# A hybrid decoder trunk: four plain tiles for six in the first up projection, its norm under the fourth product, and a last norm from two banks

## The chip, the cores and the metric

The kernel runs on one core of a Trainium2 chip. A core has TensorE (PE, matrix products; its weight loads are shown apart as PEld), VectorE (DVE), ScalarE (ACT), GpSimd (POOL) and SyncE (SP, which issues transfers). Each engine works through its own list of instructions in the order in which they were written down; semaphores make one engine wait for another. Transfers (DMAs) are issued by SP, POOL or ACT and run beside the engines. The metric is the device time of one execution in microseconds (us), taken as the median of several runs. All times below are microseconds unless they are marked ns.

## The reference

One layer over 512 positions of width 1024, batch 1, everything in float32:

```python
x = x + 0.5 * swiglu(rmsnorm(x, ffn1_norm), ffn1_wg, ffn1_wu, ffn1_wd)
x = x + hybrid_mixer(rmsnorm(x, mix_norm), ...)
x = x + 0.5 * swiglu(rmsnorm(x, ffn2_norm), ffn2_wg, ffn2_wu, ffn2_wd)
return rmsnorm(x, final_norm)

def rmsnorm(x, g):
    return x * lax.rsqrt(jnp.mean(x * x, axis=-1, keepdims=True) + EPS) * g

def swiglu(x, w_gate, w_up, w_down):      # w_gate, w_up: 1024 x 2816, w_down: 2816 x 1024
    return (jax.nn.silu(x @ w_gate) * (x @ w_up)) @ w_down
```

The mixer (sparse attention, a gated recurrence, two merge gates and an output projection) is not touched by the change. The final norm is.

## The kernel before

**Numbers in two parts.** Every float32 operand is split into a rounded part (`h`, made by ACT) and the rest (`l`, made by DVE as the difference, `wsplit`). A product of two such operands is three matmuls: h by h, h by l, l by h (`mm3`). The rounded type is `F32R`.

**The first up projection** works on tiles of 128 of the 2816 columns, so there are 22 tiles, each with a gate product (j = 0) and an up product (j = 1). The input lies transposed: `x[k]` holds 128 channels by 512 positions, eight of them. The first norm is not applied ahead of the products. The products take `y[k]`, which is `x[k]` by the norm's weight; the factor per position, `rstd`, is multiplied onto the results. `norm_steps` forms it: matmuls with a constant matrix `mean` on `acc` (the sum of squares, formed by ACT and DVE), a square root on ACT, a reciprocal on DVE, four transposes on PE that spread the factor over the partitions, and a copy to `rstd` by ACT.

The order is this:
1. Three products (both of tile 0, the gate of tile 1) are formed while x and their weights arrive (banks `WP`, weights `WS`), and a fourth (`pu`, the up product of tile 1) follows with weights from `AH[0]`. These banks wait until `rstd` is there; then `ffn_act` makes the activations of tiles 0 and 1.
2. `ffn_up` begins with plain tiles ("direct"). Each is two products of 8 x 3 matmuls of 512 positions (`gemm`). There are DIRECT = 4 of them, tiles 2 to 5, so eight products. With tiles 0 and 1 this makes six plain tiles (PLAIN = 6, which is also what the down projection is laid out for).
3. The other 16 tiles go in pairs through a scheme of Strassen and Winograd's kind: two tiles, two halves of the channels and two halves of the positions make a 2 x 2 problem with seven products in place of eight. Each of the seven products is 4 x 3 matmuls of 256 positions. This part is called the stream. `stream` lists its products as (p, w), with p the kind of product and w counting gate and up of each pair. Products of kinds 2, 5 and 3 are "wide" from the third w on: one weight load serves both halves of the operand.

**The operands of the stream.** Seven operands, four tiles each, are formed from the normed input and used by every pair: `n11` (for p = 1), `b21` (2), `t2` (6), `t1` (5), `r` (7), `q` (4) and `n22` (3). `moving_operands` forms them in four parts j: two scaled inputs `ca` and `cb` (DVE, with `rstd`), differences of their halves (DVE), and for each operand tile a rounded half (ACT, tile `cm`) and the rest. The rest is made in one of two ways. For n11, n22 and the last t1 and t2, DVE forms it. For the others ACT writes the negative of the source and a transfer issued by POOL adds the source onto it (`G.dma_start(..., accum_op=ALU.add)`).

**Banks.** Products 1, 6, 7 and 4 of one w add into one bank (`o.beta`), and between them `results` takes the partial sum out. After product 1, ACT copies the bank to `t1`; product 6, two places later in the stream, may add to the bank only after this copy.

**Queues around the change.** In `ffn_up` the order on every engine is written by hand (`tc.manual_schedule`). In the plain part each product is issued in two halves, and between and after the halves stand: the results of the product before (`results_direct`), the split of the weights two products ahead (`prepare_direct`), and a piece of operand forming. The stream's loop issues, for each i, `products(i)`, `results(i - 1)`, `prepare(i + LEAD)` with LEAD = 4 (the split of the weights four products ahead, and weight sums where p is 6 or 3), and at times a load. A load of one w (`load`) is four transfers on SP and two adding transfers on POOL. Raw weights have three buffers, split weights three.

**The end.** The second down projection leaves rows of 128 positions by 512 columns. Its last TAIL = 3 steps are issued for row block m = 0, then for m = 1. After them come, for each m, the addition of the last bank to the residual rows (DVE), the sum of squares (ACT for m = 0, DVE for m = 1), root, reciprocal, two scalings, and two output transfers of 128 x 512.

Of the kernel before, what the change touches and what calls it, by code (L numbers as in the profile page):

```python
# [14 lines left out]
P = 128  # L15
S = 512
# [26 lines left out]
WARM = 8  # L43
HS = S // 2
LEAD = 4
PLAIN, PAIRS, TAIL = 6, 8, 3
DIRECT = 4
WIDE, FIRST_WIDE = (2, 5, 3), 2

# [128 lines left out]
def hybrid_kernel(ctx, tc, xt, vec, w1u, w1d, wm, wki, wrg, watt, wrnn, wout, w2u, w2d, gf, out):  # L178
# [21 lines left out]
    def nm(s):  # L200
        cnt[0] += 1
        return f"{s}_{cnt[0]}"
# [34 lines left out]
    def wsplit(r, h, l):  # L237
        A.activation(h, r, AF.Copy)
        V.tensor_sub(l, r, f(h))
# [77 lines left out]
    def moving_operands(g):  # L317
# [28 lines left out]
        for j in range(KD // 2):  # L346
# [20 lines left out]
            moved("q", q)  # L367
            yield

    def ffn_act(pg, pu):  # L370
# [7 lines left out]
    def ffn_up(y, wu, n0, hs, g, waiting=(), given=(), ahead=None):  # L378

# [2 lines left out]


        H = KD // 2 * P
        f0 = n0 + DIRECT
        count = KF - f0
        ws = []

# [60 lines left out]
        stream = []  # L451
        for w in range(count):
            stream += [(1, w), (2, w)] + [(4, w - 1)] * (w > 0) + [(6, w)]
            stream += [(3, w - 1)] * (w > 0) + [(5, w), (7, w)]
        w = count - 1
        stream[-3:] = [(5, w), (7, w), (3, w - 1), (4, w), (3, w)]
        units = []
# [47 lines left out]

        def wide(p, w):

            return p in WIDE and FIRST_WIDE <= w < count - 2 * (p != 2)

        def results(i):  # L510
            p, w = stream[i]
# [25 lines left out]
            elif p == 3:  # L537
# [7 lines left out]
                else:  # L545
                    A.activation(o.t1, o.t1, AF.Silu)

        with tc.manual_schedule(engines=ENGINES):
            for _ in range(len(raws), RAWS + len(raws)):
                fetch()  # L550
            together(prepare_direct(), prepare_direct())
            operands, norm = moving_operands(g), norm_steps(acc)
            for d, (n, j) in enumerate(direct):
                sums.append(psum(("aux", "mm")[n % 2]))
                if d == 1:
                    norm_rest(norm)
                    hs.extend(ffn_act(*p) for p in waiting)
                gemm(sums[d], split_[d], y, range(KD), last=False, upto=KD // 2)
                steps = [results_direct(d - 1)] if d else []
                if d + 2 < len(direct):  # L560
                    together(prepare_direct(), *steps)
                    fetch()
                else:
                    together(*steps)
                    for i in range(2):
                        prepare(2 * (d + 2 - len(direct)) + i)
                if d == 0:
                    for _ in range(3):
                        next(norm)
                if d in (4, 6):  # L570
                    load_ = load(len(ws))
                if d >= 4:
                    next(load_, None)
                if d > 1:
                    next(operands, None)
                gemm(sums[d], split_[d], y, range(KD), first=False, since=KD // 2)
                if d > 1:
                    next(operands, None)
            for _ in operands:
# [200 lines left out]
    for r, src in zip(AH, (w1u[1, 1], w1u[2, 0], w1u[2, 1], w1u[3, 0])):  # L780
        Q.dma_start(r, src)

    def given(r):
        h, l = (wsp.tile([P, WMAX], F32R, tag=t, name=nm(t)) for t in ("wh", "wl"))
        wsplit(r, h, l)
        return h, l

    y = []
    for k in range(KD):
        y.append(norm_tile(k, V_G1, False))  # L790
        if k % CH == 0:
            c = slice(k * P, (k + CH) * P)
            for r, h, l in WS:
                wsplit(r[:, c], h[:, c], l[:, c])
        for i in range(3):
            mm3(WP[i], WS[i][1:], slice(k * P, (k + 1) * P), y[k], k == 0, k == KD - 1)
    pu, w = psum(), given(AH[0])
    for k in range(KD):
        norm_sum(k)
    gemm(pu, w, y, range(KD))  # L800
    hs = []

    sums = []
    d1 = block_down(hs, w1d, sums)
    ffn_up(y, w1u, 2, hs, V_G1, ((WP[0], WP[1]), (WP[2], pu)), AH[1:], d1.tasks_at)

    cc = const.tile([P, 8], F32, name="cc")
    hb = vt[:, V_BX:V_BX + 8]
# [802 lines left out]
            banks[key] = psum("aux" if p == 2 else "mm")  # L1611
        return banks[key]

    def products(i, ms=range(2)):
        h, l = (t[:, i % 2 * S:(i % 2 + 1) * S] for t in units[i // 2])
# [12 lines left out]
        t, starts = turned[p, j], p in (1, 2, 5)  # L1628
        opens = dict(skip_group_check=not starts)
        for m in ms:  # L1630
            o, th, tl = chain(p, m), t[:, m * QB:(m + 1) * QB], t[:, HS + m * QB:HS + (m + 1) * QB]
            T.matmul(o, th, h, start=starts and j == 0, stop=False, **opens)
# [81 lines left out]
    ffn_up(y2, w2u, 0, hs, V_G2, ahead=tasks_at)  # L1714
    with tc.manual_schedule(engines=ENGINES):
        assert min(d2.tasks) >= 0
        for i in range(len(steps) - TAIL):
# [11 lines left out]
        results(len(steps) - TAIL - 1)  # L1729
        assert not late  # L1730

        for m in range(2):
            for i in range(len(steps) - TAIL, len(steps)):
                products(i, (m,))
        for m in range(2):
            r = rows(m, 1)
            if m:
                norm_root(0)
            V.scalar_tensor_tensor(r, chain(4, m), 0.5, r, op0=ALU.mult, op1=ALU.add)
            squares(m, 1, norms[m][:, 2:3], (A, V)[m])  # L1740
        scaled(0, nc.scalar)
        norm_root(1)
        scaled(1, nc.scalar)


def _tiles(w, kt, m=P):
# [55 lines left out]
```

## Time and profile before

| | |
|---|---|
| median of 3 runs | 1063.96 us (1063.28 to 1064.0) |
| profiled execution | 1063.79 us |
| its span, first to last instruction | 1062.0 us |
| PE busy | 1052.5 us, 99% of the span |
| DVE, ACT, POOL busy | 83%, 63%, 16% |
| first matmul of the three first products | 4.85 us |
| rstd written by ACT | 35.88 us |
| first matmul of the first stream | 73.79 us |
| first matmul of the first down projection | 234.34 us |
| last matmul issued | 1054.28 us |

How to read the rows that follow later. A row of a timeline has the start in us from the beginning of the span, the length in us, the engine, the line of the kernel (L172 is the helper through which nearly every instruction is written, so the names of the tiles tell more than the line), the operation, what it writes <- what it reads, the shapes, and xN where N like instructions in a row were merged. In square brackets stands how long the engine was idle ahead of it and which work ended that wait. Matmuls overlap, so the distance between two starts is what one costs, not its length. A row of windows has the stretch, its length, PE's busy time (and instructions), the clock that PE was granted as a share of the full one, the share of the transfer engines in use, and GB/s. Buffer names have no numbers: `cm` is any operand tile of the stream, `wh` and `wl` the two parts of split weights, `tg` and `h` what the results are taken into, `ca` and `cb` the scaled inputs.

### The profile page before, as it was taken

The page shows a single profiled execution, that of the slowest core. Times are in us where ns is not written, and L with a number is a line of the kernel's source. Part 1 is how long each engine was busy: PE and PEld are TensorE (multiplying, and loading weights), DVE is VectorE, ACT ScalarE, POOL GpSimd, SP SyncE. Part 2 cuts the span into 40 slices and gives each one's busy share as a digit, 9 for nine tenths or more (in the row PEclk, how much of TensorE's full clock was granted, in tenths as well). Part 3 has the DMA queues.
Part 4 walks back from the last instruction along what each step waited for, and adds up shares of the span by engine and source line. Part 5 has one row for each costly group of instructions (what it writes and reads, how often), then busy time and mean ns, then how long its engine had stood idle before and what let it go on. Part 6 is the DMA issues. An engine that isn't in the chain of part 4 may idle for free.

```text
span 1062.0 us, 17140 instructions
## 1 busy us (share of the span) xinstructions
PE 1052.5 (99%) x6068; PEld 926.2 (87%) x6068; DVE 879.4 (83%) x1734; ACT 665.3 (63%) x1311; POOL 171.5 (16%) x219
## 2 busy tenths in 40 slices
PE   9999999999999999999999999999999999999997
PEld 7889999999999888888888888888899999998885
DVE  6687898889978889899989867756878988878885
ACT  6575555555656668897896574446656555565753
POOL 0161111102430002110100000001611111101510
PEclk9999999999999999999999999999999999999999
DMA  7297677738993464343423211434977777548973
GB/s 279 60 258 184 175 197 175 186 107 235 259 206 97 132 172 124 105 124 106 138 80 99 81 31 54 143 112 110 247 188 172 189 197 165 154 120 257 256 160 120
DMA packets 73239, 165.98 MB, mean 156 GB/s; under 512 B 9024, under 2 KB 15296, under 8 KB 73152
## 3 DMA queue, kind: packets, MB, share of 16 engines
q1 hardware_dynamic: 46608, 119.72, 34.7%
q0 software_dynamic: 26112, 44.58, 24.2%
q8 instruction: 48, 0.79, 0.3%
q10 hardware_dynamic: 432, 0.57, 0.2%
q14 instruction: 39, 0.32, 0.1%
HBM read 151.73 MB, written 2.10 MB: 145 GB/s over the span
## 4 chain that ended last, share of the span: by engine, by line
PE 98%; DMA 0%; issue 0%; ACT 0%; DVE 0%; SPq 0%; ACTq 0%
PE mm L172 68%; PE aux L172 29%; DMA x<-xt 0%; ACT wh L172 0%; ACT yh L172 0%; SPq L160 0%; DVE o L172 0%; DVE yl L172 0%; DVE xr L172 0%; DVE acc L172 0%; DVE sq L172 0%; ACT sq L172 0%; DVE rs L172 0%; ACTq L172 0%; DVE ss L172 0%
## 5 line engine op out<-in xcount | busy, mean ns | idle before, releaser
L172 PE MATMUL mm<-cm,wh 128*128 128x256 f32 x1472 | 268.5, 283 | 0.0
L172 PEld LDWEIGHTS mm<-cm,wh 128*128 128x128 f32 x1472 | 229.1, 191 | 3.4 <-ACT tg L172 0.2
L172 DVE TENSOR_TENSOR wl<-wr,wh 128x512 fp32r<-128x512 f32 (+2 forms) x228 | 188.9, 832 | 45.9 <-ACT wh L172 44.2
L172 PE MATMUL mm<-cm,wl 128*128 128x256 f32 x736 | 208.4, 283 | 0.0
L172 ACT ACTIVATE wh<-wr 128x512 fp32r<-128x512 f32 (+3 forms) x230 | 167.9, 737 | 56.6 <-issue 21.5
L172 PE MATMUL mm<-yh,wh 128*128 128x512 f32 (+1 forms) x416 | 163.7, 394 | 0.7 <-ACT wh L172 0.7
L172 PE MATMUL mm<-yl,wh 128*128 128x512 f32 (+1 forms) x416 | 162.3, 390 | 0.0
L172 PE MATMUL aux<-cm,wh 128*128 128x512 f32 (+1 forms) x552 | 159.6, 351 | 0.0
L172 PE MATMUL mm<-yh,wl 128*128 128x512 f32 x408 | 159.2, 390 | 0.0
L172 PEld LDWEIGHTS mm<-cm,wl 128*128 128x128 f32 x736 | 140.4, 191 | 0.0
L172 ACT ACTIVATE wh<-s 128x512 fp32r<-128x512 f32 x152 | 92.9, 624 | 54.4 <-DVE s L172 42.1
L172 DVE TENSOR_TENSOR wl<-s,wh 128x512 fp32r<-128x512 f32 x152 | 103.5, 686 | 24.9 <-ACT wh L172 23.2
L172 PE MATMUL aux<-cm,wl 128*128 128x256 f32 x440 | 123.7, 281 | 0.0
L172 PEld LDWEIGHTS aux<-cm,wh 128*128 128x128 f32 x552 | 96.7, 189 | 12.8 <-DMA cm<-cb 0.2
L172 PEld LDWEIGHTS mm<-yh,wh 128*128 128x128 f32 (+1 forms) x416 | 77.9, 187 | 17.8 <-ACT wh L172 1.4
L172 PEld LDWEIGHTS mm<-yl,wh 128*128 128x128 f32 (+1 forms) x416 | 77.6, 187 | 16.0 <-DVE yl L172 0.8
L172 PEld LDWEIGHTS mm<-yh,wl 128*128 128x128 f32 x408 | 76.6, 188 | 16.5 <-DVE wl L172 0.2
L172 PEld LDWEIGHTS aux<-cm,wl 128*128 128x128 f32 x440 | 83.5, 190 | 0.0
L172 PE MATMUL mm<-wh,cm 128*128 128x512 f32 x192 | 59.1, 389 | 0.0
L172 ACT ACTIVATE tg<-tg 128x512 f32<-128x512 f32 (+1 forms) x44 | 24.1, 548 | 50.8 <-DVE tg L172 50.8
L160 POOL DMA_DIRECT2D s<-w2u x36 | 33.6, 1063 | 125.1 <-DVE wl L172 47.0
L160 POOL DMA_DIRECT2D cm<-cb x8 | 7.1, 888 | 266.3 <-DMA wr<-w2u 209.1
(243 smaller groups left out, 2063.7 us busy)
## 6 DMA issues: line engine op xcount, KB each, us to landing
wr<-wm SPq DMA_DIRECT2D x39, 512.0 KB, 3.6
wr<-w2u SPq DMA_DIRECT2D x26, 512.0 KB, 4.7
wr<-w1u SPq DMA_DIRECT2D x21, 512.0 KB, 5.4
wr<-w1d SPq DMA_DIRECT2D x18, 512.0 KB, 4.4
s<-w2u SPq DMA_DIRECT2D x36, 256.0 KB, 6.0
s<-w2u POOLq DMA_DIRECT2D x36, 256.0 KB, 5.1
wr<-w2d SPq DMA_DIRECT2D x18, 512.0 KB, 5.4
s<-w1u SPq DMA_DIRECT2D x32, 256.0 KB, 5.7
```

The lines of the kernel that those rows point to most:

```text
L160: return self.engine.dma_start(out, src, **kw)
L172: return call(*args, **kw)
```

## The change

- The last two slices of the three first products are issued bank by bank: both slices of the first bank, then both of the second, then of the third.
- The fourth product moves into `ffn_up` (`first_tiles`). The mean's matmuls stand ahead of it, the transposes in its middle.
- There are two direct tiles in place of four (`plain` = 2), so four plain tiles in all and 18 in the stream. The loads of the first two w are issued ahead of the plain products.
- The operands are formed by `operand_parts` in the order of use: n11, b21, t2 and t1 in four parts among the plain products (the activations of tiles 0 and 1 among them, `act_steps`), then r, q and n22, one tile at a time, the first three behind the last plain product's halves and the others one for each i of the stream's loop. r and q are now subtracted in place from `ca` and `cb`.
- The stream takes the gate and the up of the first pair together: 1, 2, 6, 5 of each, then 7, 4 and 3 of both.
- At the end four steps are left for the tail. Row block 1 is formed in halves of 256 columns; the four steps of the second half go to a bank of their own (`rest`). Additions, sums of squares and scalings of row block 1 are issued by halves, and its last output is two transfers.

```diff
-PLAIN, PAIRS, TAIL = 6, 8, 3
+PLAIN, PAIRS, TAIL, TAIL2 = 6, 8, 3, 4
...
+    def operand_parts(g):
...
+        def moved(name, src, soon=False):
+            o = rounded(name, src)
+            if soon:
+                V.tensor_sub(o[:, hi], src, f(o[:, lo]))
+                return
+            A.activation(o[:, hi], src, AF.Copy, scale=-1.0)
+            G.dma_start(o[:, hi], src, accum_op=ALU.add)
+
+        def negated(name, src):
+            o = rounded(name, src, -1.0)
+            V.scalar_tensor_tensor(o[:, hi], src, -1.0, f(o[:, lo]), op0=ALU.mult, op1=ALU.subtract)
...
+        def first(j):
...
+            for o, k in ((p.a, j), (p.b, j + KD // 2)):
+                V.scalar_tensor_tensor(o, x[k], col(g, k), rstd, op0=ALU.mult, op1=ALU.mult)
+            moved("b21", p.b[:, lo])
+            yield
+            V.tensor_sub(p.a[:, hi], p.a[:, hi], p.a[:, lo])
+            V.tensor_sub(p.t, p.b[:, hi], p.a[:, hi])
+            negated("n11", p.a[:, lo])
+            last = j == KD // 2 - 1
+            moved("t2", p.t, last)
+            moved("t1", p.a[:, hi], last)
+            yield
+
+        def rest():
+            for n, p in enumerate(parts):
+                V.tensor_sub(p.a[:, lo], p.a[:, lo], p.t)
+                moved("r", p.a[:, lo], n == 3)
+                yield
+            for n, p in enumerate(parts):
+                V.tensor_sub(p.b[:, lo], p.b[:, lo], p.t)
+                moved("q", p.b[:, lo], n == 3)
+                yield
+            for p in parts:
+                negated("n22", p.b[:, hi])
+                yield
...
+        if begin:
+
+            stream, w1 = [(p, w) for w in range(2) for p in (1, 2, 6, 5)] + [(p, w) for p in (7, 4, 3) for w in range(2)], 2
...
-            return p in WIDE and FIRST_WIDE <= w < count - 2 * (p != 2)
+            return p in WIDE and FIRST_WIDE + 2 * bool(begin) <= w < count - 2 * (p != 2)
...
+        def first_tiles():
+
+            pu, r = begin
+            fetch()
+            loads(2)
+            norm = norm_steps(acc)
+            h, l = (wsp.tile([P, WMAX], F32R, tag=t, name=nm(t)) for t in ("wh", "wl"))
+            next(norm)
+            wsplit(r, h, l)
+            next(norm)
+            ready_ = prepare_direct(), prepare_direct()
+            next(ready_[0])
+            next(norm)
+            gemm(pu, (h, l), y, range(KD), last=False, upto=KD // 2)
+            together(*ready_)
+            norm_rest(norm)
+            gemm(pu, (h, l), y, range(KD), first=False, since=KD // 2)
...
+            some(2)
+            for d, (n, j) in enumerate(direct):
+                sums.append(psum(("aux", "mm")[n % 2]))
+                gemm(sums[d], split_[d], y, range(KD), last=False, upto=KD // 2)
+                steps = [results_direct(d - 1)] if d else []
+                if d + 2 < len(direct):
+                    together(prepare_direct(), *steps)
+                    fetch()
+                else:
+                    together(*steps)
+                    for i in range(2):
+                        prepare(2 * (d + 2 - len(direct)) + i)
+                some((1, 1, 1, 0)[d])
+                gemm(sums[d], split_[d], y, range(KD), first=False, since=KD // 2)
+                some((2, 2, 2, 2)[d])
+            return work_
...
                 if i + LEAD < len(stream):
                     prepare(i + LEAD)
+                    if begin:
+                        next(operands, None)
...
         for i in range(3):
-            mm3(WP[i], WS[i][1:], slice(k * P, (k + 1) * P), y[k], k == 0, k == KD - 1)
-    pu, w = psum(), given(AH[0])
+            for k_ in (k,) if k < KD - 2 else range(KD - 2, KD) if k == KD - 1 else ():
+                mm3(WP[i], WS[i][1:], slice(k_ * P, (k_ + 1) * P), y[k_], k_ == 0, k_ == KD - 1)
...
-    ffn_up(y, w1u, 2, hs, V_G1, ((WP[0], WP[1]), (WP[2], pu)), AH[1:], d1.tasks_at)
+    ffn_up(y, w1u, 2, hs, V_G1, ((WP[0], WP[1]), (WP[2], pu)), AH[1:], d1.tasks_at, 2, (pu, AH[0]))
...
+        tail = range(len(steps) - TAIL2, len(steps))
+        for i in tail:
+            products(i, (0,))
+        for i in tail:
+            products(i, (1,), lo)
+        rest = psum("aux")
+        for i in tail:
+            products(i, (1,), hi, rest)
...
+        V.scalar_tensor_tensor(r, chain(4, 1), 0.5, r, op0=ALU.mult, op1=ALU.add)
+        V.tensor_tensor_reduce(sq[:, lo], r[:, lo], r[:, lo], 1.0, 0.0, ALU.mult, ALU.add, ss[:, 2:3])
+        V.scalar_tensor_tensor(ss[:, 1:2], ss[:, 2:3], 1.0 / D, ss[:, 1:2], op0=ALU.mult, op1=ALU.add)
...
+        V.scalar_tensor_tensor(r[:, hi], rest[:, hi], 0.5, r[:, hi], op0=ALU.mult, op1=ALU.add)
+        V.tensor_tensor_reduce(sq[:, hi], r[:, hi], r[:, hi], 1.0, 0.0, ALU.mult, ALU.add, ss[:, 2:3])
+        V.tensor_scalar(o1, o1, rs, None, op0=ALU.mult)
...
+        for q, h in enumerate((lo, hi)):
+            V.scalar_tensor_tensor(o1[:, h], r[:, h], rs, gb[1][:, h], op0=ALU.mult, op1=ALU.mult)
+            Q.dma_start(c[:, S + q * HS:S + (q + 1) * HS], o1[:, h])
```

In `first_tiles`, `some(n)` issues the next n of these pieces, in this order: the first half of tile 0's activation; part 0's scaled inputs and b21 with the second half of that activation; the rest of part 0; part 1 in two pieces; the first half of tile 1's activation; part 2's scaled inputs and b21 with the second half of that; the rest of part 2; part 3 in two pieces; then r, q and n22, one tile a piece.

More of the change, by code (lines that the diff above doesn't have):

```diff
@@ L368, in moving_operands, with place, rounded @@
             yield
+    def operand_parts(g):
+        moving.update((n, []) for n in ("n11", "b21", "t2", "t1", "r", "q", "n22"))
+        held, parts, taken = [], [], []
+        def place():
+            if len(moving["n11"]) > 1 and not taken:
+                taken.append(True)
+                for k in ("pth", "ptl"):
+                    t = ptp.tile([P, NQ * S], F32R, tag=k, name=nm("cm"))
+                    held.extend(t[:, i * S:(i + 1) * S] for i in range(NQ))
+            return held.pop(0) if held else slot(F32R, "cm")
+        def rounded(name, src, sign=1.0):
+            o = place()
+            moving[name].append(o)
+            A.activation(o[:, lo], src, AF.Copy, scale=sign)
+            return o
+        def moved(name, src, soon=False):
[8 more added lines that the diff above has]
+            V.scalar_tensor_tensor(o[:, hi], src, -1.0, f(o[:, lo]), op0=ALU.mult, op1=ALU.subtract)
+        class Part:
+            pass
+        def first(j):
+            p = Part()
+            p.a, p.b = slot(F32, "ca"), slot(F32, "cb")
+            if j % 2 == 0:
+                p.pair = slot(F32, "ct")
+            else:
+                p.pair = parts[-1].pair
+            p.t = p.pair[:, (lo, hi)[j % 2]]
+            parts.append(p)
+            for o, k in ((p.a, j), (p.b, j + KD // 2)):
[21 more added lines that the diff above has]
+                yield
+        return first, rest
@@ L546, in results, with loads, pieces, some @@
                     A.activation(o.t1, o.t1, AF.Silu)
+        def loads(n):
+            for _ in range(n):
+                load_ = load(len(ws))
+                next(load_)
+                next(load_, None)
+        def first_tiles():
[14 more added lines that the diff above has]
+            gemm(pu, (h, l), y, range(KD), first=False, since=KD // 2)
+            first, rest = operand_parts(g)
+            acts = [act_steps(hs, *p) for p in waiting]
+            parts = [first(k) for k in range(KD // 2)]
+            def pieces():
+                next(acts[0])
+                yield
+                next(parts[0])
+                next(acts[0])
+                yield
+                next(parts[0])
+                yield
+                for _ in range(2):
+                    next(parts[1])
+                    yield
+                next(acts[1])
+                yield
+                next(parts[2])
+                next(acts[1])
+                yield
+                next(parts[2])
+                yield
+                for _ in range(2):
+                    next(parts[3])
+                    yield
+                yield from rest()
+            work_ = pieces()
+            def some(n):
+                for _ in range(n):
+                    next(work_, None)
+            some(2)
[6 more added lines that the diff above has]
+                    fetch()
+                else:
+                    together(*steps)
[5 more added lines that the diff above has]
+            return work_
@@ L554, in ffn_up @@
+            for d, (n, j) in enumerate(direct) if not begin else ():
                 sums.append(psum(("aux", "mm")[n % 2]))
@@ L578, in ffn_up @@
                     next(operands, None)
-            for _ in operands:
+            for _ in operands if not begin else ():
                 pass
@@ L781, in hybrid_kernel @@
         Q.dma_start(r, src)
[L783 to L786, printed above, removed]
     y = []
@@ L1612, in chain, with products @@
         return banks[key]
-    def products(i, ms=range(2)):
-        h, l = (t[:, i % 2 * S:(i % 2 + 1) * S] for t in units[i // 2])
+    def products(i, ms=range(2), cols=slice(0, S), bank=None):
+        h, l = (t[:, i % 2 * S:(i % 2 + 1) * S][:, cols] for t in units[i // 2])
         if steps[i][0] == "D":
@@ L1629, in products @@
         opens = dict(skip_group_check=not starts)
+        first = j == PAIRS - TAIL2 if bank is not None else starts and j == 0
         for m in ms:
-            o, th, tl = chain(p, m), t[:, m * QB:(m + 1) * QB], t[:, HS + m * QB:HS + (m + 1) * QB]
-            T.matmul(o, th, h, start=starts and j == 0, stop=False, **opens)
+            o, th, tl = (chain(p, m) if bank is None else bank)[:, cols], t[:, m * QB:(m + 1) * QB], t[:, HS + m * QB:HS + (m + 1) * QB]
+            T.matmul(o, th, h, start=first, stop=False, **opens)
             T.matmul(o, tl, h, start=False, stop=False, **opens)
@@ L1716, in hybrid_kernel @@
         assert min(d2.tasks) >= 0
-        for i in range(len(steps) - TAIL):
+        for i in range(len(steps) - TAIL2):
             if i < KD // 2:
```

61 lines of the change are left out of this document (37 added, 24 removed).

## The prediction

> **What bounds the kernel now.** I read the page's busy times and the chain that ended last, then the timelines of PE, DVE and ACT around the places that change, then the end.
>
> ```profile
> PE 1052.5 (99%) x6068; PEld 926.2 (87%) x6068; DVE 879.4 (83%) x1734; ACT 665.3 (63%) x1311; POOL 171.5 (16%) x219
> PE 98%; DMA 0%; issue 0%; ACT 0%; DVE 0%; SPq 0%; ACTq 0%
> 41.31 10.88 PE mm L172 x48
> 80.17 2.88 PE mm L172 x24
> ```
>
> PE is the bound from one end to the other: whatever work it gains or loses, and every hole opened in it, goes straight into the time. The last two rows (chain of waits, in order of time) price its work: 48 matmuls of 512 columns took 10.88, so a plain product of 24 takes 5.44; 24 matmuls of 256 columns took 2.88, so a stream product of 12 takes 1.44. DVE and ACT cost nothing as long as they stay ahead, and that is what has to be checked where the operands of the stream are formed. PE's own timeline there, and the rows of ACT and of the weight load that end its one hole:
>
> ```profile
> 31.62 1.05 PE L172 MATMUL aux<-mean,acc 128*128 128x128 f32 x8
> 32.43 0.48 PE L172 MATMUL aux<-yh,wh 128*128 128x512 f32 x1
> 35.24 0.60 PE L172 MATMUL aux<-ident,rs 128*128 128x128 f32 x4
> 35.60 0.48 PE L172 MATMUL aux<-yh,wh 128*128 128x512 f32 x1
> 73.79 0.40 PE L172 MATMUL mm<-cm,wh 128*128 128x256 f32 x2
> 76.30 0.57 PE L172 MATMUL aux<-cm,wh 128*128 128x256 f32 x2
> 77.02 0.50 PE L172 MATMUL mm<-cm,wh 128*128 128x256 f32 x2
> 75.88 0.68 DVE L172 TENSOR_TENSOR h<-mm,rstd 128x512 f32<-128x512 f32 x1
> 76.08 0.62 ACT L172 ACTIVATE wh<-s 128x512 fp32r<-128x512 f32 x1
> 76.61 0.37 ACT L172 ACTIVATE tg<-mm 128x256 f32<-128x256 f32 x1
> 77.02 0.30 PEld L172 LDWEIGHTS mm<-cm,wh 128*128 128x128 f32 x2 [0.24 <-ACT tg L172]
> ```
>
> The stream starts at 73.79; its third product (operand t2) should start two products later, at 76.67, and starts at 77.02: 0.35 lost. It adds into the bank in which the first product lies, so it has to wait until ACT has copied that bank out (76.61 + 0.37 = 76.98). The copy was late because ACT, which works in order, stood behind operand forming. This small hole is the one to watch: in the changed kernel the same copy stands in the same place of ACT's queue.
>
> **The change part by part.**
>
> *Plain products.* Two tiles go from plain to the stream: 4 products of 5.44 go (-21.74), 14 of 1.44 come (+20.16). The wide products stay as many, since their first pair moves with the tiles. Net -1.58.
>
> *Before the plain products.* Its rows:
>
> ```profile
> 18.98 1.48 DVE L172 TENSOR_TENSOR acc<-acc,sq 128x512 f32<-128x512 f32 x2
> 21.72 2.96 ACT L172 ACTIVATE wh<-ahead 128x1024 fp32r<-128x1024 f32 x3 [3.36 <-PE mm L172]
> 23.33 0.39 PE L172 MATMUL mm<-yl,wh 128*128 128x512 f32 x1
> 23.78 0.50 PE L172 MATMUL aux<-yh,wh 128*128 128x512 f32 x1
> ```
>
> The three first products end at 23.1. ACT may split the fourth's weights only when the first product frees its buffer; finishing each bank over both last slices frees it some 1.3 earlier, so the hole at 23.33-23.78 (0.22, and 0.1 of slow restart) goes: -0.33. The mean's matmuls (32.43 - 31.62 = 0.81) and the transposes (0.36) are moved, not removed; the sum they read is ready at 20.5. Then PE: mean to 23.9, half of the fourth product to 26.7, transposes, rstd by ACT at about 27.9 (36.51 before), fourth product done near 30.2, four plain products to 51.6. The stream so starts 22.2 earlier.
>
> *DVE under that.* From 27.9 to 51.6 it has 23.7. Its prices, from one start to the next:
>
> ```profile
> 36.51 0.69 DVE L172 TENSOR_TENSOR tg<-mm,rstd 128x512 f32<-128x512 f32 x1 [3.33 <-ACT rstd L172]
> 37.12 0.68 DVE L172 TENSOR_TENSOR h<-mm,rstd 128x512 f32<-128x512 f32 x1
> 43.40 1.23 DVE L172 TENSOR_TENSOR wl<-wr,wh 128x1024 fp32r<-128x1024 f32 x1
> 44.54 0.68 DVE L172 TENSOR_TENSOR h<-h,tg 128x512 f32<-128x512 f32 x1
> 45.14 0.75 DVE L172 SCALAR_TENSOR_TENSOR ca<-x,vt,rstd 128x512 f32<-128x512 f32 x1
> 45.80 0.75 DVE L172 SCALAR_TENSOR_TENSOR cb<-x,vt,rstd 128x512 f32<-128x512 f32 x1
> 46.58 0.42 DVE L172 TENSOR_TENSOR cr<-ca,cb 128x256 f32<-128x256 f32 x1
> 47.04 0.43 DVE L172 TENSOR_TENSOR ca<-ca 128x256 f32<-128x256 f32 x1
> 47.38 0.42 DVE L172 SCALAR_TENSOR_TENSOR cm<-ca,cm 128x256 fp32r<-128x256 f32 x1
> 60.59 1.22 DVE L172 TENSOR_TENSOR wl<-wr,wh 128x1024 fp32r<-128x1024 f32 x1 [1.58 <-ACT wh L172]
> 72.41 1.29 DVE L172 TENSOR_TENSOR wl<-s,wh 128x512 fp32r<-128x512 f32 x2 [0.78 <-ACT wh L172]
> ```
>
> So 0.60 for 512 columns, 1.14 for 1024, 0.66 for a scaled operand, 0.34 for 256 columns (0.46 behind its own input). Ahead of the last plain product's result it must do: two activations, 6 x 0.60 = 3.6; four steps of plain results, 2.5; two whole weight splits, 2.3; four half splits and one added weight, 3.0; four parts of the operands, each 2 x 0.66 + 0.46 + 0.34 + 0.34, 9.8; the last part's two low halves, 0.7; three of the r's, 1.0. Together 22.9, 97% of its time, if it never waits. It does wait: DVE and ACT hand work back and forth in order, and the rows show DVE idle 1.58 and 0.78 at a weight split for that reason. Following the order of issue through both queues with these prices, I get waits of 1.25 at each whole split and 0.4 to 0.8 at four other places, 4.5 in all. DVE then reaches the last plain product's result at 27.9 + 22.9 + 4.5 = 55.3, 3.8 late. (The same reckoning over the kernel before puts this result at 75.84; its row says 75.88.)
>
> *The first hole.* Then come, on DVE, the result's two multiplies and a split (to 57.7), the subtraction of the last r (0.42); only then can ACT round that r (58.1), and behind it stands the copy of the first bank: 58.45 to 58.85. The third product could start at 51.6 + 2.88 = 54.5 and starts at 58.9: 4.4 lost.
>
> *The second hole.* For each of the next four products the issue order is split (ACT, then DVE), subtraction (DVE), two roundings (ACT). ACT's prices:
>
> ```profile
> 65.52 1.14 ACT L172 ACTIVATE wh<-wr 128x512 fp32r<-128x512 f32 x2
> 66.56 0.71 ACT L172 ACTIVATE cm<-cr 128x256 fp32r<-128x256 f32 x2
> ```
>
> Two 512s end in 1.14 (0.52 and 0.62), two 256s in 0.71 (0.31 a piece). One round is a chain over both engines: ACT split 0.62, DVE split 0.60, subtraction 0.42, two roundings 0.62, and about 0.1 of hand-over: 2.36, against PE's 1.44. From the last r's rounding at 58.1, four rounds (one with another copy, 0.31) end at 68.0, and the copy of the second pair's first bank at 68.7. The product that waits for it could start four products after 58.9, at 64.7: 4.0 lost. Later rounds (n22) have no subtraction ahead of ACT; a last 0.4 is lost at one more such copy, and the LEAD of four products rebuilds. Ends for all holes: 8.3 to 9.8, by hand-overs of 0.02 or 0.08; I take 8.8.
>
> *Transfers.* The two loads are issued on SP as soon as the first raw buffers are free, near 16.5 instead of 51.7, and wanted at 46, and nothing that is wanted earlier stands behind them in its queue. POOL's four adds to them stand ahead of the first cm add at about 31, and land by then. The cm adds:
>
> ```profile
> DMA to landing us min/median/max: 3.4/6.3/8.6
> ```
>
> The last b21, issued near 49.8, lands at 53.2 to 58.4; wanted at 54.1. It may open part of the first hole, never past 58.9: no term of its own. Moving two halvings to the stream's end costs nothing: the second up projection has that form already, and PE is busy through it:
>
> ```profile
> 780.00:950.00 170.00, 170.00 (x1234) 1.00 0.67 169
> ```
>
> *The end.*
>
> ```profile
> 1054.28 0.39 PE L172 MATMUL mm<-wl,cm 128*128 128x512 f32 x1
> 1054.71 0.69 DVE L172 SCALAR_TENSOR_TENSOR xr<-mm,xr 128x512 f32<-128x512 f32 x1
> 1055.43 0.69 DVE L172 CUSTOM_DVE_ANT_0 sq<-xr 128x512 f32<-128x512 f32 x1
> 1056.05 0.75 DVE L172 SCALAR_TENSOR_TENSOR o<-xr,rs,gb 128x512 f32<-128x512 f32 x1
> 1056.91 0.75 DVE L172 SCALAR_TENSOR_TENSOR o<-xr,rs,gb 128x512 f32<-128x512 f32 x1
> 1057.66 0.37 ACTq L1697 DMA_DIRECT2D out<-o  x1
> ```
>
> Now 2.95 of DVE lies behind PE's last result (1054.71 to 1057.66). 24 matmuls of 256 for 12 of 512 cost PE 2.88 - 2.72 = 0.16. Behind them lie 0.42 + 0.45 on 256 columns, the multiply of o1 (0.35 to 0.68), root and reciprocal, and two halves of 0.42 and 0.34: some 2.4. Gain 0.2 to 0.7; I take 0.4. The output bytes are as many, in one transfer more.
>
> *Sum.* -1.58 - 0.33 - 0.35 (the old hole) + 8.8 - 0.4 = +6.1. Profiled execution 1063.79 (span 1062.0, the rest around it); the median of the runs, 1063.96, lies 0.17 above. Forecast: 1070.0. About 0.2% (2.1) is what a measurement tells from no change.
>
> *The clock.* The windows after PE's last matmul (ended 1054.67):
>
> ```profile
> 1058.00:1059.00 1.00, 0.00 (x0) 1.00 0.85 309
> 1059.00:1060.00 1.00, 0.00 (x0) 0.51 0.96 352
> ```
>
> The granted clock fell to half 4.3 after it. My holes of 4.4 and 4.0 are of that length. The Trainium skill, "TensorE: Matmul & The Clock Gate", Part 1, says that PE is put to half clock after a whole idle window of about 3.4 us, and needs about as long a busy stretch to come back, the windows running freely; the trace's 4.3 fits. By it each hole could cost some 1.7 more (an estimate from that page), and the sum would be 1070.0 or up to 1073.4.
>
> **The rivals.**
>
> 1. *The queues keep up* (faster). If DVE and ACT did not wait for each other, DVE would be done by 50.8, ahead of 51.6. It decides at the first bank's copy: on time at 54.5, it is free; I have it 4.4 later. Then -1.58 - 0.33 - 0.35 - 0.4 = -2.7: 1061.3. For it: 22.9 does fit into 23.7. Against: the idle rows above, and that already with 32 us for this work DVE came 2.1 late (75.88 for a product done at 73.79).
> 2. *Backlog only.* DVE is late once, but the rounds of 2.36 overlap (the roundings not holding up the next split), so the second hole and the 0.4 behind it close: 1070.0 - 4.4 = 1065.6. Against: ACT works in order, as the copy at 76.61 showed.
> 3. *The clock drops in the holes.* A product at half clock takes 2.88; over the 3 us that the last rows show at half, a hole costs 1.5 more: 1071.5 for one, 1073.0 for both. For it: the two windows. Against: the holes are no longer than what it took there.
> 4. *The change does not save plain work:* the two added pairs come at less than full width. 14 x 1.44 against 21.74 leaves 1.58 only; should it vanish, 1071.6.
>
> **How the numbers follow.** Forecast with both holes, 1068 to 1071.4: 0.65. Clock or no saving, 1071.5 to 1073.2: 0.12. Backlog only, 1065 to 1068: 0.11. Queues keep up, 1061.3: 0.09; in between, within 2.1 of before: 0.03. The range 1065.5 to 1072.0 holds the first, most of the third, a part of the second: about 0.82. Slower 0.88, the same 0.03, faster 0.09.
>
> **What would show it.** PE's stream should start near 51.6; its third and seventh products should each stand behind an ACT copy tg<-mm for about 4, and DVE should start the last plain h<-mm near 55.3. POOL's row of cm adds may be named for the first hole instead. If DVE starts that multiply near 52, or the splits behind the stream's start follow each other at 1.44, the forecast is wrong, and the first rival or the second holds. At the end DVE's last o should end some 2.4 to 2.7 behind PE.

## The result and the profile after

The changed kernel takes 1070.29 us (median of 6 runs, 1069.42 to 1071.85) against 1063.76 for the kernel before (6 runs, 1063.09 to 1064.0): a ratio of 1.0063, with a 95% interval of 1.005 to 1.0076. It is 6.5 slower, and 1070.0 was forecast. The profiled execution is the slowest of the six: 1071.85, with a span of 1070.1, so 8.06 above the profiled execution of before. The readings below go by it.

The page's busy times and the shares of the chain that ended last, after:

```profile
PE 1054.0 (98%) x6152; PEld 931.6 (87%) x6152; DVE 887.5 (83%) x1759; ACT 670.4 (63%) x1326; POOL 172.5 (16%) x221
PE 93%; DVE 3%; ACT 2%; DMA 1%; issue 1%; SPq 0%; DVEq 0%; ACTq 0%
```

PE is busy 1.5 longer than before (1054.0 for 1052.5) in a span that is 8.1 longer, so most of the loss is idle PE. Its share of the chain fell from 98% to 93%: from the writing of `rstd` (27.72) to the stream's seventh product (69.00) the chain now runs over DVE and ACT, though PE itself has work until 55.07. The waits of PE (total, times, longest) say where:

```profile
PE mm L172 <- ACT tg L172: 4.2, 1, 4.2
PE mm L172 <- ACT tu L172: 2.4, 1, 2.4
...
PE aux L172 <- ACT wh L172: 0.2, 1, 0.2
...
```

The first two lines are new. Both are copies of a bank's first product, one for each w of the first pair (the second goes to a tile called `tu`). PE's timeline at the beginnings of products, and of what lies around them:

```profile
23.46 0.72 PE L172 MATMUL aux<-mean,acc 128*128 128x128 f32 x5
52.03 0.40 PE L172 MATMUL mm<-cm,wh 128*128 128x256 f32 x2
59.27 0.80 PE L172 MATMUL mm<-cm,wh 128*128 128x256 f32 x2 [4.20 <-ACT tg L172]
62.00 0.58 PE L172 MATMUL aux<-cm,wh 128*128 128x256 f32 x2
63.60 0.40 PE L172 MATMUL mm<-cm,wh 128*128 128x256 f32 x2
66.36 0.28 PE L172 MATMUL aux<-cm,wl 128*128 128x256 f32 x1
69.00 0.62 PE L172 MATMUL mm<-cm,wh 128*128 128x256 f32 x2 [2.36 <-ACT tu L172]
71.56 0.63 PE L172 MATMUL aux<-cm,wh 128*128 128x256 f32 x2
73.47 0.40 PE L172 MATMUL mm<-cm,wh 128*128 128x256 f32 x2
242.20 0.40 PE L172 MATMUL aux<-hh,wh 128*128 128x512 f32 x1
```

Read by starts, the stream begins 21.76 earlier than before (52.03 for 73.79). Its third product starts at 59.27, where 52.03 + 2.88 = 54.91 was possible: the first hole is 4.36. The third product takes 62.00 - 59.27 = 2.73 and not 1.44, the fourth 63.60 - 62.00 = 1.60: together 1.45 too much. The seventh could follow at 66.48 and starts at 69.00: the second hole is 2.52. The seventh and the eighth take 2.56 and 1.91. The first down projection then begins at 242.20, 7.86 later than before, so nearly the whole loss lies in front of it. From the stream's start to there it is 190.17 instead of 160.55, so 29.62 more: 20.16 for the 14 added products, less 0.35 for the old hole that went, and the remaining 9.8 are holes and slow products. A further 0.5 is lost by the end of the last down projection, which shows a wait for late weights (the last line of the waits) that the profile of before does not have.

The slow products have their reason in the clock. Windows of PE (stretch, length, busy time and instructions, granted clock, share of the transfer engines, GB/s):

```profile
56.00:60.00 4.00, 0.73 (x3) 0.87 0.46 66
60.00:64.00 4.00, 4.00 (x27) 0.70 0.17 25
64.00:68.00 4.00, 2.64 (x23) 1.00 0.52 75
68.00:72.00 4.00, 3.00 (x15) 0.65 0.85 130
```

PE ran at half clock from about 59.0 to 62.4 and again from 69.2 to 72.6 (a mean clock of 0.87 over 4.00 is 1.0 at half, at the end of that window; narrower windows give the same edges). What held the copies up is seen on the chain of waits, in order of time (start, length, what), from the last plain product's result to the second copy:

```profile
57.47 0.69 DVE wl L172
58.16 0.35 DVE ca L172
...
58.53 0.42 ACT cm L172
...
61.70 0.53 ACT wh L172
...
62.25 0.69 DVE wl L172
62.94 0.35 DVE cb L172
...
63.31 0.72 ACT cm L172 x2
64.04 0.27 ACT tg L172
...
68.58 0.37 ACT tu L172
...
69.00 2.76 PE mm L172 x12
```

Here the path leaves PE altogether and goes round between two engines: split on ACT, split on DVE, subtraction on DVE, two roundings on ACT, and again. DVE's rows of the same stretch give the length of a round and the lateness it began with:

```profile
55.80 0.68 DVE L172 TENSOR_TENSOR h<-mm,rstd 128x512 f32<-128x512 f32 x1
62.25 0.69 DVE L172 TENSOR_TENSOR wl<-s,wh 128x512 fp32r<-128x512 f32 x1 [0.97 <-ACT wh L172]
64.86 0.69 DVE L172 TENSOR_TENSOR wl<-s,wh 128x512 fp32r<-128x512 f32 x1 [1.58 <-ACT wh L172]
67.20 0.69 DVE L172 TENSOR_TENSOR wl<-s,wh 128x512 fp32r<-128x512 f32 x1 [1.31 <-ACT wh L172]
```

DVE starts the last plain result 3.77 after the stream's start (55.80 - 52.03). Its splits then follow each other at 2.61 (with one more copy on ACT, at 64.04 in the chain) and 2.34, where PE wants one each 1.44.

The end, on DVE; PE's last matmul ended at 1063.20:

```profile
1063.23 0.42 DVE L172 SCALAR_TENSOR_TENSOR xr<-aux,xr 128x256 f32<-128x256 f32 x1
...
1064.69 0.88 DVE L172 SCALAR_TENSOR_TENSOR o<-xr,rs,gb 128x256 f32<-128x256 f32 x2
```

The last scaling ends at 1065.57, which is 2.37 behind PE; before it was 2.99 (1057.66 - 1054.67).

### The profile page after: what moved, and what is told of

Same layout as the page of the kernel before. It is cut to its first block, busy times and chain, and to the rows that moved or that the text cites. A ratio compares the mean times of both kernels' runs of the same rounds, so it can differ in the third digit from the quotient of the medians.

```text
span 1070.1 us, 17353 instructions
## 1 busy us (share of the span) xinstructions
PE 1054.0 (98%) x6152; PEld 931.6 (87%) x6152; DVE 887.5 (83%) x1759; ACT 670.4 (63%) x1326; POOL 172.5 (16%) x221
## 4 chain that ended last, share of the span: by engine, by line
PE 93%; DVE 3%; ACT 2%; DMA 1%; issue 1%; SPq 0%; DVEq 0%; ACTq 0%
PE mm L172 66%; PE aux L172 27%; ACT cm L172 1%; DMA wr<-w2d 1%; DVE wl L172 1%; ACT wh L172 1%; DMA x<-xt 0%; DVE cb L172 0%; DVE ca L172 0%; DVE cm L172 0%; ACT yh L172 0%; DVE xr L172 0%; DVE h L172 0%; SPq L160 0%; DVE o L172 0%
## 5 line engine op out<-in xcount | busy, mean ns | idle before, releaser
L172 PE MATMUL mm<-cm,wh 128*128 128x256 f32 x1536 | 282.4, 284 | 6.6 <-ACT tg L172 4.2
L172 PEld LDWEIGHTS mm<-cm,wh 128*128 128x128 f32 x1536 | 240.7, 192 | 10.1 <-ACT tg L172 4.4
L172 PE MATMUL mm<-cm,wl 128*128 128x256 f32 x768 | 218.5, 285 | 0.0
L172 PE MATMUL aux<-cm,wh 128*128 128x512 f32 (+1 forms) x600 | 168.6, 347 | 0.0
L172 PE MATMUL mm<-yl,wh 128*128 128x512 f32 (+1 forms) x400 | 156.0, 391 | 0.1
L172 PEld LDWEIGHTS mm<-cm,wl 128*128 128x128 f32 x768 | 147.6, 192 | 0.0
L172 PE MATMUL aux<-cm,wl 128*128 128x256 f32 x464 | 130.7, 282 | 0.0
L172 PEld LDWEIGHTS aux<-cm,wh 128*128 128x128 f32 x600 | 104.8, 191 | 12.5
L172 PE MATMUL mm<-wh,cm 128*128 128x512 f32 (+1 forms) x192 | 58.1, 385 | 0.0
L160 POOL DMA_DIRECT2D s<-w1u x36 | 32.0, 987 | 149.7 <-DMA s<-w1u 71.1
```

The source lines that it names most:

```text
L160: return self.engine.dma_start(out, src, **kw)
L172: return call(*args, **kw)
```

## The experiments

The theory to be tested: the loss lies in the first up projection alone; DVE's backlog makes the first hole, and the round over DVE and ACT makes the second. Against it stood a late adding transfer on POOL as the cause of the first hole, and the clock as the real price of both.

**One half of the change alone.** The first kernel is the kernel before with only the new end; the second is the changed kernel with the old end.

```diff
 # kernel before, with the new end only
-PLAIN, PAIRS, TAIL = 6, 8, 3
+PLAIN, PAIRS, TAIL, TAIL2 = 6, 8, 3, 4
...
+        rest = psum("aux")
+        for i in tail:
+            products(i, (1,), hi, rest)
...
```

> The kernel before with the new end alone (four tail steps, the second half of row block 1 in a bank of its own, additions, squares and scalings by halves); the first up projection stays as before. My theory: PE's last matmul comes 0.16 later, 2.4 of DVE behind it in place of 2.95, so 0.4 faster than before (0.2 to 0.7). Rival: the end is set by the output transfers, which carry as many bytes, and nothing changes (within 0.1).

> The changed kernel with the old end: only the first up projection is changed. My theory: the whole loss and more is here, 0.4 above the changed kernel, some 6.7 above before. Rival (the loss lies partly at the end): at or below the changed kernel.

New end alone: 1063.2 (11 runs) against 1063.63 (27 runs of before), ratio 0.9996 (0.9987 to 1.0005). The shift of -0.4 is the size forecast, but the interval takes in no change. The profile does show the mechanism. PE's last matmul and DVE's last scaling:

```profile
1055.17 0.28 PE L172 MATMUL aux<-wl,cm 128*128 128x256 f32 x1
1056.94 0.88 DVE L172 SCALAR_TENSOR_TENSOR o<-xr,rs,gb 128x256 f32<-128x256 f32 x2
```

It ends 2.37 behind PE (1057.82 - 1055.45) as in the changed kernel. The front alone: 1069.9 (4 runs), ratio 1.0058 (1.0043 to 1.0073), with the same holes of 4.2 and 2.4 in its waits. The whole loss comes from the front; what the end gives is too small for these runs. The front alone was expected 0.4 above the changed kernel and came 0.4 below it, a difference that these runs do not tell from none.

**All but the exchange of tiles.** The changed kernel with four plain tiles in the loop as before, so six in all, and the operand pieces dealt out over eight plain products.

```diff
-                some((1, 1, 1, 0)[d])
+                some((1, 1, 1, 0, 0, 0, 0, 0)[d])
...
-                some((2, 2, 2, 2)[d])
+                some((2, 2, 2, 2, 2, 2, 2, 0)[d])
...
-            return p in WIDE and FIRST_WIDE + 2 * bool(begin) <= w < count - 2 * (p != 2)
+            return p in WIDE and FIRST_WIDE <= w < count - 2 * (p != 2)
...
-    ffn_up(y, w1u, 2, hs, V_G1, ((WP[0], WP[1]), (WP[2], pu)), AH[1:], d1.tasks_at, 2, (pu, AH[0]))
+    ffn_up(y, w1u, 2, hs, V_G1, ((WP[0], WP[1]), (WP[2], pu)), AH[1:], d1.tasks_at, 4, (pu, AH[0]))
```

> The changed kernel with six plain tiles again (four direct tiles, 16 in the stream, the same tiles wide as before); the fourth product with the norm under it, operands in order of use and the new end stay. My theory: the order of use and the early norm do no harm, the time does: with four more plain products (21.7) DVE is ahead again, both holes close, and what is left of the change is the old small holes gone (0.33 and 0.35) and the end (0.4): about 1.0 below before, near 1062.9. Rival (the order of use itself, or the paired order of the stream, makes the holes): holes of some 4 to 8 stay, 1066 to 1070.

1062.24 (11 runs), ratio 0.9988 (0.9979 to 0.9997): faster than both kernels, by 1.4 than the one before. PE's waits have neither copy any more:

```profile
PE aux L172 <- DVE epst L172: 1.1, 1, 1.1
PE aux L172 <- DVE acc L172: 0.2, 1, 0.2
```

PE's rows, first and third product of its stream:

```profile
73.33 0.40 PE L172 MATMUL mm<-cm,wh 128*128 128x256 f32 x2
76.21 0.44 PE L172 MATMUL mm<-cm,wh 128*128 128x256 f32 x2
```

The stream starts 0.46 earlier than before, and the third product 2.88 behind the first: the old hole of 0.35 is gone. With 0.62 - 0.16 = 0.46 for the end these make 1.27 of the 1.4. So the rest of the change, taken together, pays; the exchange of tiles costs 1070.29 - 1062.24 = 8.05, where 1.58 was to be saved by it.

**The round, without the backlog.** In the changed kernel each subtraction of an r or q is issued one piece ahead of its rounding, so that ACT does not wait for it.

```diff
             for n, p in enumerate(parts):
                 V.tensor_sub(p.a[:, lo], p.a[:, lo], p.t)
-                moved("r", p.a[:, lo], n == 3)
+                if n:
+                    moved("r", parts[n - 1].a[:, lo])
                 yield
             for n, p in enumerate(parts):
                 V.tensor_sub(p.b[:, lo], p.b[:, lo], p.t)
-                moved("q", p.b[:, lo], n == 3)
+                if n:
+                    moved("q", parts[n - 1].b[:, lo])
+                else:
+                    moved("r", parts[3].a[:, lo], True)
                 yield
+            moved("q", parts[3].b[:, lo], True)
```

> The changed kernel with each subtraction of r and q issued one piece ahead of its rounding; nothing else is moved, and the work is the same. My theory: ACT's rounding then no longer waits for a subtraction that stands behind the weight split just made, so the rounds fall from 2.36 to under PE's 1.44, the second hole closes and the first shrinks by about 1.5; no half clock behind a second hole: some 5.5 below the changed kernel, near 1064.8. Rival 1 (DVE's backlog alone makes the holes): the same work, so within 1 of the changed kernel. Rival 2 (the POOL adds of r and q come too late): they start later still, so slower than the changed kernel.

1065.85 (10 runs), ratio 1.0021 (1.0012 to 1.003): 4.4 less than the changed kernel. PE's wait for `tu` is gone, and the first hole has shrunk. The timeline of PE and DVE:

```profile
51.22 0.40 PE L172 MATMUL mm<-cm,wh 128*128 128x256 f32 x2
54.98 0.68 DVE L172 TENSOR_TENSOR h<-mm,rstd 128x512 f32<-128x512 f32 x1
56.93 0.50 PE L172 MATMUL mm<-cm,wh 128*128 128x256 f32 x2 [2.68 <-ACT tg L172]
```

The backlog is as it was (54.98 - 51.22 = 3.76, after 3.77). From DVE's multiply to the third product it is now 1.95 instead of 3.47, since the last r's rounding no longer stands between; the hole is 3.76 + 1.95 - 2.88 = 2.83. The second hole fell with the round: DVE's splits now start at 59.45, 60.44 and 62.03, which is 0.99 and 1.59 apart. This separates the two causes: the order of issue made the second hole and a third of the first. What is left is the backlog, and a clock drop behind it. The windows of PE:

```profile
56.00:60.00 4.00, 3.07 (x18) 0.76 0.67 96
60.00:64.00 4.00, 4.00 (x29) 0.81 0.58 88
```

The half clock lasts from 58.1 to 61.5 here. It began 1.2 after PE had gone back to work. No later hole hides it: the third and fourth product take 4.36 for 2.88, so 1.48 more, which the expected 1064.8 left out.

**POOL's transfer.** The last b21's low half is formed by DVE in place of the transfer issued by POOL.

```diff
-            moved("b21", p.b[:, lo])
+            moved("b21", p.b[:, lo], j == KD // 2 - 1)
```

> The changed kernel with the low half of the last b21 formed by DVE instead of a transfer issued by POOL; all else as it is. My theory: the transfer does not set the end of the first hole, so nothing is gained; the one subtraction more on the late DVE (0.34, and a wait for ACT) makes both holes end some 0.5 to 0.8 later: 0 to 1 above the changed kernel, 1070 to 1071. Rival (the POOL add lands late and makes the first hole): the hole shrinks by 1 to 4 and the time falls by as much.

1070.98 (4 runs), ratio 1.0068 (1.0054 to 1.0082): no gain. The waits of PE:

```profile
PE mm L172 <- ACT tg L172: 4.9, 1, 4.9
PE mm L172 <- ACT tu L172: 2.2, 1, 2.2
```

More work on DVE makes the first hole longer: DVE starts the last plain result 4.50 behind the stream's start (56.29 - 51.79), 0.73 later than in the changed kernel, and the third product starts 7.97 behind it, also 0.73 later. The transfer is not its cause.

**The clock alone.** In the changed kernel 18 and 16 spare matmuls on the constant `mean`, into a bank that nobody reads, are issued ahead of the stream's third and seventh product (each shows as two records of PE, so the 18 are the x36 below). They give PE work in the holes and leave the queues of DVE and ACT as they were.

```diff
+IDLE = {2: 18, 6: 16}
...
             for i in range(len(stream)):
+                if begin and i in IDLE:
+                    for _ in range(IDLE[i]):
+                        T.matmul(spare[:, :P], mean, mean, start=True, stop=True)
                 products(i)
```

> The changed kernel with 18 spare matmuls (128 columns, a constant, into a bank that nobody reads) ahead of the stream's third product and 16 ahead of its seventh, so that PE works through most of both holes. Theory (half clock behind the second hole is paid, behind the first it is hidden by the second): PE keeps full clock, the queues are not touched, so the third and seventh product start where they did (59.3 and 69.0), and 1.4 goes: about 1.4 below the changed kernel, near 1069. Rival (the clock costs nothing that counts): as the changed kernel, or up to 1 slower where the spare matmuls outlast a hole.

1069.29 (5 runs, 1068.98 to 1070.07), ratio 1.0055 (1.0042 to 1.0067). PE's timeline and, behind it, its windows:

```profile
51.34 0.40 PE L173 MATMUL mm<-cm,wh 128*128 128x256 f32 x2
54.21 4.18 PE L173 MATMUL aux<-mean 128*128 128x128 f32 x36
58.56 0.51 PE L173 MATMUL mm<-cm,wh 128*128 128x256 f32 x2 [0.17 <-ACT tg L173]
...
68.29 0.51 PE L173 MATMUL mm<-cm,wh 128*128 128x256 f32 x2
```

```profile
60.00:64.00 4.00, 4.00 (x36) 1.00 0.23 33
68.00:72.00 4.00, 3.86 (x33) 1.00 0.67 103
```

The clock now stays full. Yet the third product starts 7.22 behind the stream's start and the seventh 16.95, against 7.24 and 16.97 in the changed kernel: the queues set both times, and the first half clock cost nothing, since the time it took from PE would have been a longer second hole. With the clock held full that hole, filled here by the spare matmuls, is 68.29 - 58.56 - 4 x 1.44 = 3.97. Only the second was paid, 1.0 by the medians. The intervals of the two ratios overlap, so that figure is not separated from none by these runs; in the profile of the changed kernel the seventh and the eighth product took 4.47 for 2.88, which is 1.59 more.

**The backlog alone.** With the subtractions ahead, DVE also gets three instructions of 512 columns less ahead of the last plain result: tile 1's activation is left out but for one Silu which ACT reads from the bank.

```diff
     def act_steps(hs, pg, pu):
+        if pg is WP[2]:
+            tu = slot(F32, "h")
+            A.activation(tu, pg, AF.Silu)
+            yield
+            hs.append(tu)
+            yield
+            return
         tg, tu = work("tg"), slot(F32, "h")
```

> The kernel with the subtractions a piece ahead, and tile 1's activation left out but for the activation function itself, read from the bank by ACT (three DVE multiplications of 0.60 go; ACT has as many instructions). What is computed for tile 1 is therefore not the reference's. Theory (what is left of the first hole, 2.7, is DVE's backlog): it shrinks by 1 to 1.8 to about 1.3, and with it, if it is short enough, the half clock behind it (1 to 1.5): 1.2 to 3 below the kernel with the subtractions ahead, so 1063 to 1064.7. Rival (the hole is set by ACT or by the POOL adds): within 0.5 of that kernel.

1063.5 (10 runs), ratio 0.9999 (0.999 to 1.0008): 2.35 less than with the subtractions ahead alone. The timeline of PE and DVE:

```profile
51.33 0.40 PE L172 MATMUL mm<-cm,wh 128*128 128x256 f32 x2
53.37 0.68 DVE L172 TENSOR_TENSOR h<-mm,rstd 128x512 f32<-128x512 f32 x1
55.32 0.50 PE L172 MATMUL mm<-cm,wh 128*128 128x256 f32 x2 [0.96 <-ACT tg L172]
```

DVE is 2.04 late instead of 3.76, so 1.72 less, and the hole is 55.32 - 51.33 - 2.88 = 1.11 instead of 2.83, also 1.72 less. Backlog on DVE goes into the first hole one for one, and behind this hole the clock did not drop, as the windows of PE show:

```profile
56.00:60.00 4.00, 4.00 (x36) 1.00 0.41 59
60.00:64.00 4.00, 4.00 (x36) 1.00 0.90 117
```

At full clock too the second hole stays closed: the seventh product follows without a wait. Only a later product waits 0.36 for a copy to `tu`, at 68.91. This is not a usable kernel; it shows what DVE's load at this place is worth.

Not tried: four plain tiles without any hole. Even with the three instructions gone DVE was 2.04 late, which speaks for taking work off DVE there; whether that, or another order of its work, reaches it stays open.

## Why the prediction was right, point by point

The sum came out within 0.3 of the median, and the loss came by the mechanism that was named. Not all its terms came out: that the sum lies so close is partly luck, since a cost that was left out (the clock) and one that did not come (a later copy) stood against each other. The terms below are read from the profiled execution, which is 1.56 above the median.

- *Plain products, -1.58.* Held, by starts: 20.16 for the added products, the holes and the slow products account for the stream's excess to within 0.1. PE's busy time agrees: -1.58, +0.16 at the end and 3.04 of slow products make +1.6, and it grew by 1.5. Rival 4 is out.
- *Start hole, -0.33.* Held: the mean's matmuls follow the last first product without a gap, at 23.46. That this is 0.36 behind the 23.1 of the forecast is when the first products ended, and it varies from one execution to the next: the stream started at 52.03 here and between 51.2 and 51.8 in the profiles of five variants. The forecast's own steps miss by as much: a fourth product done near 30.2 and four of 5.44 make 51.96, not 51.6.
- *DVE's backlog, 3.8 late at 55.3.* Held: 3.77 late, at 55.80. So rival 1, by which the queues keep up, is out. The last experiment shows that it is the backlog which sets what the new order leaves of the hole.
- *First hole, 4.4.* Held: 4.36.
- *Rounds of 2.36.* Held: 2.34, and 2.61 with a copy.
- *Second hole, 4.0.* Mis-sized in the profile: 2.52. The step that failed is "the product that waits for it could start four products after 58.9". It took four products at 1.44 for granted; the third and the beginning of the fourth ran at half clock, so PE came 1.45 later to the place where the queues held it up in any case. The distance from the third to the seventh product was forecast as 9.8 and was 9.73: the queues' side of the reckoning was right, PE's was not. With the clock held full the hole is 3.97, the 4.0 of the forecast.
- *The last 0.4 at another copy.* Absent from the waits of the changed kernel.
- *The clock.* Left out of the sum, given as a rival of one or two added costs of 1.5. Here the prediction was wrong in kind: it measured its holes against the 4.3 that the clock took to fall at the end of the kernel before, but the clock fell behind both, and 2.36 was enough. All six runs had a mean granted clock of 0.995, against 0.998 or 0.999 before, so this was the common case. But only the second drop cost anything (1.59 in the profile). Term by term, in the profile, 4.36 + 1.45 + 2.52 + 1.59 make 9.9 against 8.8 forecast for the holes. The first drop's 1.45 and the 1.5 that the second hole lacks are the same time; what is left is 1.59 too little for the second drop against 0.4 too much for the later copy. The profiled execution alone, at 1071.85, fits the rival of one drop (1071.5) better than the forecast; the median fits the forecast.
- *The end, -0.4.* In the profiles the last scaling lies 0.62 nearer to PE, less 0.16 of added matmuls. By the times it cannot be told from nothing: the end alone gave -0.4, and the changed kernel with the old end was 0.4 faster, not slower, than with the new one.
- *Transfers at nothing.* Held: taking the last b21 off POOL did not shorten the hole. The other transfers were not tried one by one, but none is named in PE's waits.

Rival 2 (the rounds overlap, 1065.6) was the time of another kernel: with subtractions one piece ahead the rounds did overlap, and it ran in 1065.85. The match is partly chance: the first hole was smaller there than the rival has it, and a clock drop made up for it.

## What to carry to other kernels

Before you exchange work on the busiest engine for cheaper work, count the time that the exchange takes away from the engines that prepare what comes next: here 21.74 of plain products were the cover for forming the operands, and 1.58 saved on PE cost 8. When two engines that work in order hand pieces back and forth, price the whole round and not each engine's load; here issuing the dependent step one piece later closed the second hole at no cost in work. And keep the copy of a bank that PE waits for clear of work that is wanted later: from DVE's last plain result to the third product it was 3.47 with a subtraction and its rounding in front of the copy, and 1.95 without.

## What the runs showed of the hardware

PE's clock fell after shorter holes than expected, and later than the hole. The holes of 2.36 (after), 2.20 (b21 by DVE) and 2.68 (subtractions ahead) were each followed by a granted clock of 0.50, while 0.96 (less on DVE) was not. The fall came 2.6 to 5.0 after PE's last matmul, in three cases after PE had been back at work for 0.2, 0.6 and 1.2. Each lasted about 3.4, and within one execution two falls lay at whole multiples of that: 59.0 and 69.2 in the changed kernel, 59.8 and 70.1 with b21 on DVE, three steps of 3.4 apart. The Trainium skill, "TensorE: Matmul & The Clock Gate", Part 1, describes windows of about 3.4 us that run freely; the grid agrees. It names a whole idle window as the condition, and there the measurement differs: counted back from its end at 69.2, the window before the second fall was idle for 2.36 of 3.4, and PE worked in the rest. With b21 on DVE it was 2.20, with the subtractions ahead 2.24 (54.69 to 56.93). Which share of a window decides is not settled by these runs, nor is the 0.96 hole a bound, since it may have lain across two windows.

The runs of the changed kernel spread over 2.4, those with the clock held full over 1.1. That the place of the holes in these windows makes this spread is not shown: the 27 runs of the kernel before, which has no such holes, spread over 1.9.
